# Strassen products of a feed-forward layer accumulated onto one another in PSUM

## The chip, the cores and the metric

The kernel runs on one core of a Trainium2 chip. The metric is the device time of one execution in microseconds (us). Five engines take part: TensorE (PE in the profile; its weight loads are PEld), VectorE (DVE), ScalarE (ACT), GpSimd (POOL) and SyncE (SP), which issues the transfers.

## The reference

One layer of a streaming encoder: a half-step feed-forward, token mixers, a second half-step feed-forward and a final norm, over 1024 + 64 tokens of width 1024. The change touches only the feed-forward parts:

```python
def swiglu(h, w_up, w_down):
    a, b = jnp.split(h @ w_up, 2, axis=-1)
    return (jax.nn.silu(a) * b) @ w_down
...
    x = x + 0.5 * g1 * swiglu(modulate(rms_norm(x, norm_f1), sh1, sc1), w_up1, w_down1)
...
    x = x + 0.5 * g2 * swiglu(modulate(rms_norm(x, norm_f2), sh2, sc2), w_up2, w_down2)
```

D_FF is 2816, that is 22 blocks of 128 columns each in `a` and in `b`.

## The kernel before, in words

**Numbers.** All products are in fp32 precision made from two parts: each operand is split into `hi` (a cast on ScalarE, line 134) and `lo` (source minus hi, line 138, on VectorE or GpSimd), and `mm3` issues three matmuls, hi·hi, hi·lo, lo·hi (lines 162, 163, 164).

**Stages.** FFN1 takes the span up to about 890 us, the mixers and their merge up to about 1870 us, FFN2 the rest. Each feed-forward runs over two groups of tokens, g = 0 (512 tokens, in halves of c = 256 columns) and g = 1 (576 tokens, c = 288).

**up(j).** For each of the 22 blocks j, `up(j)` computes a 2x2 block product in Strassen's (Winograd's) form: seven products, 0 to 6, of 12 matmuls each (4 steps k, three matmuls each). Its weights come from `pair_weights`: two blocks are loaded, sums of their halves formed (`ws` tiles), and four sets split: `wa` from the loaded block, `ws` and `wt` from the sums, `wb` from half a block. In the profile all are called whi and wlo (whi<-raw is wa; whi<-ws is ws or wt) except wb. Three buffers each exist for whi and wlo. The lists LOES say which engine makes each lo part: in both feed-forwards VectorE makes those of ws and wt, and GpSimd those of wa and of the down weights (`wd`). Each product is put into a PSUM bank of its own (pool misc, 6 banks; a tile here is called misc), and `add` (line 510, VectorE) combines the banks with tiles in SBUF called t: seven adds `t<-misc,t`, a copy of product 0 on ScalarE (line 577), two Silu on ScalarE (lines 586 and 593, SBUF to SBUF), and two multiplications `v<-t` of two SBUF tiles, also at line 510.

**down.** After every second block `down` multiplies two finished blocks with two blocks of w_down (wd) into banks (pools acc, 2 banks, and misc) and adds each to x on VectorE (line 632). 512 columns per matmul in g = 0, 288 in g = 1.

**Order.** The code's order is not the engines' order: a scheduler places the instructions on each engine's queue ahead of the run, and each engine works its queue in order, waiting on semaphores. PSUM banks go to whatever tile comes next when free.

Of the kernel before, what the change touches and what calls it, by code (L numbers as in the profile page):

```python
# [26 lines left out]
NF = DFF // P  # L27
# [16 lines left out]
NY, NV, NTT, SIDE0, SIDE, TAIL, SLACK, NRA, NS0, WAIT, NNEAR = 4, 2, 8, 7, 3, 2, 5, 3, 3, 1, 2  # L44
# [39 lines left out]
def encoder_layer(tc: tile.TileContext, a, o, stage=9):  # L84
    nc = tc.nc
# [18 lines left out]
    def slot(i):  # L104

        return hpool.tile([P, 1152], F32R, tag=f"h{i}", name=f"h{i}")
# [25 lines left out]
    def split(src, hi, lo, eng=None):  # L132

        nc.scalar.copy(hi, src)  # L134
        if eng is None:
            rr[0] += 1
            eng = nc.gpsimd if rr[0] % 3 else nc.vector
        eng.tensor_tensor(out=lo, in0=src, in1=hi.bitcast(F32), op=ALU.subtract)  # L138

    def wraw():  # L140
        return wpool.tile([P, KT, P], F32, tag="raw", name="raw", bufs=2)
# [14 lines left out]
    def load_cols(w, c0):  # L156
        return load_w((w[:, c0:c0 + P].rearrange("(k p) c -> p k c", p=P), lambda t: t))

    def mm3(out, w, x, first, last):

        (wh, wl), (xh, xl) = w, x
        nc.tensor.matmul(out, wh, xh, start=first, stop=False)  # L162
        nc.tensor.matmul(out, wh, xl, start=False, stop=False)  # L163
        nc.tensor.matmul(out, wl, xh, start=False, stop=last)  # L164

    V, G = nc.vector, nc.gpsimd
    LOE, SE = [], []
# [146 lines left out]
    def group(n):  # L314

        g = n // 2
        b0 = BLK[n][0] - GRP[g][0]
        return g, slice(b0, b0 + BLK[n][1])
# [147 lines left out]
    def run(*gens):  # L466
        for g in gens:
            for _ in g:
                pass
# [36 lines left out]
    def flat(t):  # L506
        return t.rearrange("p k c -> p (k c)")

    def add(out, in0, in1, op=ALU.add, eng=nc.vector):
        eng.tensor_tensor(out=out, in0=in0, in1=in1, op=op)  # L510
# [23 lines left out]
    def products(g, hs, ws, bank, pump):  # L534

        c = GRP[g][1] // 2

        def product(i):
            t = bank()[:, :c]
            (wh, wl), half = ws[i]  # L540
            for k in range(4):
                mm3(t, (wh[:, 4 * half + k], wl[:, 4 * half + k]), [q[:, k * c:(k + 1) * c] for q in hs[i]], k == 0, k == 3)
            pump(i)
            return t

        return product
# [7 lines left out]
    def up_weights(w_up, j):  # L554
        return pair_weights(w_up, j * P, DFF + j * P, lambda: kviews(fraw()[:, :D]), new_ws)

    def ffn(g, x, hs, w_up, w_down, gate, fpool, npool, after, after_n, side=iter(()), tail=(), first=None):

        G = 2
        gs = {}  # L560
        ln = GRP[g][1]
        c = ln // 2

        def tmp():
            return npool.tile([P, 288], F32, tag="t", name="t", bufs=NTT)[:, :c]

        def up(j, n):

            def pump(i):
                for _ in range(n * (i + 1) // 7 - n * i // 7):  # L570
                    next(side, None)

            early = j == 0 and first is not None
            ws = first if early else up_weights(w_up, j)
            product = products(g, hs, ws, misc, pump)
            p1, u2, u4 = tmp(), tmp(), tmp()
            nc.scalar.copy(p1, product(0))  # L577
            y0, t = p1, None
            if early:
                t, y0 = product(2), tmp()  # L580
                add(y0, product(3), p1)
            add(u2, product(1), p1)
            add(u4, product(2) if t is None else t, u2)
            if not early:
                add(y0, product(3), p1)
            nc.scalar.activation(y0, y0, AF.Silu)
            c22, u3 = tmp(), u2
            p7 = product(4)
            add(c22, p7, u4)
            add(u3, p7, u2)  # L590
            y1 = u4
            add(y1, product(5), u4)
            nc.scalar.activation(y1, y1, AF.Silu)  # L593
            c21 = u3
            add(c21, product(6), u3)
            v = npool.tile([P, 576], F32, tag="v", name="v", bufs=NV)
            add(v[:, c:ln], c22, y1, ALU.mult)
            add(v[:, :c], c21, y0, ALU.mult)
            gt = slot(14 + j % 3) if j % 3 < 2 else fpool.tile([P, 1152], F32R, tag="g", name="g", bufs=1)
            gs[j] = gt[:, :ln], gt[:, ln:2 * ln]  # L600
            if j < NF - 1:
                split(v[:, :ln], *gs[j], nc.gpsimd)
                return
            for cs in (slice(c, ln), slice(0, c)):
                hi, lo = (t[:, cs] for t in gs[j])
                (nc.scalar.copy if cs.start else nc.vector.tensor_copy)(hi, v[:, cs])
                nc.vector.tensor_tensor(out=lo, in0=v[:, cs], in1=hi.bitcast(F32), op=ALU.subtract)

        def down(js, last):
            wd = []  # L610
            for j in js:
                raw = wraw()
                nc.sync.dma_start(flat(raw), w_down[j * P:(j + 1) * P, :])
                w = [fpool.tile([P, KT, P], F32R, tag=f"wd{i}", name="wd", bufs=2) for i in range(2)]
                split(raw, *w, LOE[4])
                wd.append(w)
            work = [iter(tail)]
            if last:
                parts = [(n, group(n)[1]) for n in BGRP[g]]
            else:  # L620
                parts = [(None, slice(c0, c1)) for c0, c1 in ([(0, 512)] if g == 0 else [(0, 288), (288, 576)])]
            items = [(n, cs, m) for n, cs in parts for m in range(KT)]
            for q0, q1 in [(0, 6)] * last + [(q, q + 1) for q in range(6 * last, len(items))]:
                banks = [(acc if m % 4 == 0 else misc)()[:, :cs.stop - cs.start] for n, cs, m in items[q0:q1]]
                for i, j in enumerate(js):
                    for t, (n, cs, m) in zip(banks, items[q0:q1]):
                        mm3(t, (wd[i][0][:, m], wd[i][1][:, m]), [q[:, cs] for q in gs[j]], i == 0, i == len(js) - 1)
                for t, (n, cs, m) in zip(banks, items[q0:q1]):
                    for s, c0, c1 in ((0, cs.start, min(cs.stop, 512)), (1, max(cs.start, 512), cs.stop)):
                        if c0 < c1:  # L630
                            xm = x()[:, m, c0:c1]
                            nc.vector.scalar_tensor_tensor(out=xm, in0=t[:, c0 - cs.start:c1 - cs.start],  # L632
                                                           scalar=gate()[:, m, s:s + 1], in1=xm,
                                                           op0=ALU.mult, op1=ALU.add)
                    if last:
                        after(n, m)
                        for _ in range(TAIL):
                            while work and next(work[0], work) is work:
                                work.pop(0)
                    if last and m == KT - 1:  # L640
                        work.append(iter(after_n(n)))
            return chain(*work)

        groups = [list(range(j, min(j + G, NF))) for j in range(0, NF, G)]
        pend = None
        for js in groups:
            for q, j in enumerate(js):
                up(j, SIDE0 if j < NS0 and not g else SIDE)
                if q == 0 and pend is not None:
                    down(pend, False)  # L650
                    pend = None
            pend = js
        run(side)
        return down(pend, True)

# [83 lines left out]
    hs = [None] * 7  # L739
# [19 lines left out]
    first = up_weights(a["w_up1"][0], 0)  # L759
# [50 lines left out]

    args = a["w_up1"][0], a["w_down1"][0], lambda: ycol["g1"], fpool, npool, after1, lambda n: ()
    run(ffn(0, lambda: xg[0], hs, *args, side_work(), fetch_sums(hs, far1), first))
    new_x(1)
    w_in, early_w = a["w_in"][0], {}
# [36 lines left out]
    def c4():  # L851
        return dec["pool"].tile([P, dec["c4"]], F32, tag="c4", name="c4", bufs=NC4)
# [433 lines left out]
    def fill(g, mt, dst):  # L1286

        fs = ft(), ft()
        yield from pair(g, mt, mt + 1, *fs)
        for f, d in zip(fs, dst):  # L1290
            nc.sync.dma_start(part2(d, GRP[g]), f[:, :GRP[g][1]])
# [9 lines left out]
    for g in range(2):  # L1301
# [38 lines left out]
        rest = deque(fills)  # L1340
# [6 lines left out]
        while lins or rest:  # L1347
            if lins and live[0] + lins[0][0] <= dec["u"]:
                n, f, i = lins.popleft()
                live[0] += n  # L1350
                gen = f(g, i)
            elif rest:
                gen = fill(g, *rest.popleft())
# [15 lines left out]
    if stage == 2:  # L1369
        for h in range(HEADS):  # L1370
            t = c4()
            nc.sync.dma_start(t, osp_a[h])
            nc.sync.dma_start(o["dbg_x"][:, h], t)
            t = c4()
# [101 lines left out]
    hs = [None] * 7  # L1476
# [90 lines left out]
```

## Time and profile before

| | |
|---|---|
| time, median of 3 runs | 2633.03 us (2632.71 to 2633.3) |
| profiled execution | 2635.21 us, span 2633.4 us, mean granted clock 0.974 |
| busy, share of the span | PE 94%, PEld 87%, DVE 76%, POOL 62%, ACT 41% |
| matmuls | 17278 |

The span runs from the first to the last instruction of the profiled execution; its time of 2635.21 us is 1.8 us longer. Busy time counts instructions in work. The granted clock is the share of the full TensorE clock that the chip gave.

### The profile page before, as it was taken

To read this page: it belongs to the slowest core of one execution; us is meant where nothing else is said; L and a number is where in the kernel's file an instruction comes from. 1 tells how busy PE (TensorE), PEld (TensorE's weight loads), DVE (VectorE), ACT (ScalarE), POOL (GpSimd) and SP (SyncE) were. 2 spreads that over 40 slices of the span, in tenths; PEclk is the share of its full clock that TensorE was granted. 3 is DMA by queue.
4 is the path that set the end of the run, shared out by engine and by line. 5 is a ranking of instruction groups with operands and counts; after the bars stand their busy time and mean duration, and the time that the engine had idled before them with its cause. 6 is when DMAs were issued, how large, how long until landed. Compare 5 with 4: busy or idle time off the path is not lost. (4 is left out here: it accounts for less than half of the span.)

```text
span 2633.4 us, 45325 instructions
## 1 busy us (share of the span) xinstructions
PE 2483.8 (94%) x17278; PEld 2278.7 (87%) x17278; DVE 2000.4 (76%) x3276; ACT 1074.2 (41%) x1715; POOL 1630.4 (62%) x977
## 2 busy tenths in 40 slices
PE   6999998999999879998999999999799999999998
PEld 3788888999999768887888887799699998999998
DVE  6787778877667898888765665546888888877776
ACT  4443334343333443444434435534343444333333
POOL 4787666777665656677444543656767665665663
PEclk9999999999999889999999999999799999999999
DMA  8654445444443553444333335646533335323321
GB/s 274 217 179 147 153 145 182 134 144 145 137 126 111 173 163 119 155 137 127 108 111 100 120 95 182 219 129 189 158 97 100 109 106 171 120 89 91 94 82 44
DMA packets 423853, 360.78 MB, mean 137 GB/s; under 512 B 19676, under 2 KB 359316, under 8 KB 423636
## 3 DMA queue, kind: packets, MB, share of 16 engines
q1 hardware_dynamic: 423456, 357.83, 43.7%
q8 instruction: 136, 2.23, 0.4%
q14 instruction: 81, 0.66, 0.1%
q10 hardware_dynamic: 180, 0.06, 0.0%
HBM read 303.50 MB, written 52.10 MB: 135 GB/s over the span
## 5 line engine op out<-in xcount | busy, mean ns | idle before, releaser
L162 PE MATMUL misc<-h,whi 128*128 128x288 f32 (+2 forms) x3360 | 1013.3, 302 | 38.8 <-DVE t L510 18.8
L164 PE MATMUL misc<-h,wlo 128*128 128x288 f32 (+2 forms) x3360 | 987.8, 295 | 9.4 <-DVE wlo L138 8.9
L163 PE MATMUL misc<-h,whi 128*128 128x288 f32 (+2 forms) x3360 | 991.6, 295 | 4.3 <-DVE h L138 4.3
L162 PEld LDWEIGHTS misc<-h,whi 128*128 128x128 f32 x3360 | 647.2, 193 | 90.0 <-DVE t L510 28.5
L164 PEld LDWEIGHTS misc<-h,wlo 128*128 128x128 f32 x3360 | 646.4, 193 | 17.6 <-DVE wlo L138 10.2
L163 PEld LDWEIGHTS misc<-h,whi 128*128 128x128 f32 x3360 | 647.8, 193 | 13.2 <-DVE h L138 6.1
L510 DVE TENSOR_TENSOR t<-misc,t 128x256 f32<-128x256 f32 (+1 forms) x736 | 307.5, 432 | 263.1 <-PE misc L164 239.2
L138 POOL TENSOR_TENSOR wlo<-raw,whi 128x1024 fp32r<-128x1024 f32 x150 | 373.7, 2491 | 200.7 <-ACT whi L134 179.7
L138 DVE TENSOR_TENSOR wlo<-ws,whi 128x1024 fp32r<-128x1024 f32 x178 | 331.6, 1863 | 71.9 <-ACT whi L134 71.8
L138 POOL TENSOR_TENSOR wd<-raw,wd 128x1024 fp32r<-128x1024 f32 x88 | 210.8, 2416 | 152.1 <-ACT wd L134 152.1
L510 POOL TENSOR_TENSOR ws<-raw 128x512 f32<-128x512 f32 x134 | 193.3, 1445 | 123.8 <-DVE wlo L138 81.8
L134 ACT CAST whi<-ws 128x1024 fp32r<-128x1024 f32 x178 | 186.4, 1047 | 176.8 <-PE misc L163 116.1
L632 DVE SCALAR_TENSOR_TENSOR x<-misc,gate,x 128x64 f32<-128x64 f32 (+3 forms) x540 | 237.0, 483 | 23.5 <-PE misc L164 22.7
L134 ACT CAST whi<-raw 128x1024 fp32r<-128x1024 f32 x160 | 167.4, 1046 | 202.8 <-PE misc L163 158.5
L162 PE MATMUL misc<-h,wd 128*128 128x288 f32 (+3 forms) x552 | 180.9, 333 | 7.6 <-DVE t L510 6.9
L510 DVE TENSOR_TENSOR v<-t 128x288 f32<-128x288 f32 (+1 forms) x176 | 182.6, 1050 | 1.7 <-ACT t L593 1.6
L163 PE MATMUL misc<-h,wd 128*128 128x288 f32 (+3 forms) x552 | 181.7, 330 | 0.0
L164 PE MATMUL misc<-h,wd 128*128 128x288 f32 (+3 forms) x552 | 180.1, 329 | 0.0
L510 POOL TENSOR_TENSOR h<-raw 128x512 f32<-128x512 f32 x78 | 110.1, 1411 | 85.1 <-issue 40.1
L134 ACT CAST wd<-raw 128x1024 fp32r<-128x1024 f32 x88 | 88.4, 1048 | 167.7 <-PE misc L163 157.2
L162 PE MATMUL misc<-h,wb 128*128 128x256 f32 (+1 forms) x512 | 151.0, 295 | 1.9 <-ACT t L577 1.7
L163 PE MATMUL misc<-h,wb 128*128 128x256 f32 (+1 forms) x512 | 148.4, 290 | 0.0
(295 smaller groups left out, 4922.7 us busy)
## 6 DMA issues: line engine op xcount, KB each, us to landing
raw<-in_w_up_dram SPq DMA_DIRECT2D x176, 512.0 KB, 4.0
raw<-in_w_down_dram SPq DMA_DIRECT2D x88, 512.0 KB, 3.5
raw<-in_w_in_dram SPq DMA_DIRECT2D x80, 512.0 KB, 4.0
rawa<-in_w_ada_dram SPq DMA_DIRECT2D x88, 256.0 KB, 3.8
h<-in_w_ada_dram SPq DMA_DIRECT2D x16, 512.0 KB, 7.2
raw<-in_w_o_dram SPq DMA_DIRECT2D x16, 512.0 KB, 4.6
raw<-far SPq DMA_DIRECT2D x14, 576.0 KB, 3.8
rawy<-in_w_ada_dram SPq DMA_DIRECT2D x24, 256.0 KB, 5.0
```

What stands on the lines that cost most here:

```text
L134: nc.scalar.copy(hi, src)
L138: eng.tensor_tensor(out=lo, in0=src, in1=hi.bitcast(F32), op=ALU.subtract)
L162: nc.tensor.matmul(out, wh, xh, start=first, stop=False)
L163: nc.tensor.matmul(out, wh, xl, start=False, stop=False)
L164: nc.tensor.matmul(out, wl, xh, start=False, stop=last)
L510: eng.tensor_tensor(out=out, in0=in0, in1=in1, op=op)
L632: nc.vector.scalar_tensor_tensor(out=xm, in0=t[:, c0 - cs.start:c1 - cs.start], scalar=gate()[:, m, s:s + 1], in1=xm, op0=ALU.mult, op1=AL ...
```

## The change

Products that Strassen's form adds are now added by TensorE: a product may be accumulated onto a bank that already holds another. The order of the seven products becomes 0, 3, 1, 4, 2, 5, 6, in three banks: `one` takes 0, then 1, 2 and 5; `y0` takes 3; `five` takes 4, then 6. Between two products that go onto the same bank ScalarE copies the partial sum to SBUF (p1 behind 0, u2 behind 1, u4 behind 2). VectorE keeps three adds (y0 in its bank, c22 = five + u4, c21 = five + u2). Silu is applied in the bank, so the two multiplications read one SBUF tile and one bank. Line numbers move: the copies are lines 583, 593 and 602, Silu 590 and 610, the update of x 650. Block j = 0 of FFN1's first group has its weights ahead and a fourth bank.

`up` has become a generator: `begin(j + 1)` (the next block's weights and its product 0) is placed ahead of the remainder of block j.

```diff
-    def mm3(out, w, x, first, last):
+    def mm3(out, w, x, first, last, onto=False):
...
-        nc.tensor.matmul(out, wh, xh, start=first, stop=False)
+        nc.tensor.matmul(out, wh, xh, start=first, stop=False, skip_group_check=onto)
...
-        def product(i):
-            t = bank()[:, :c]
+        def product(i, t=None):
+            onto = t is not None
+            if not onto:
+                t = bank()[:, :c]
             (wh, wl), half = ws[i]
             for k in range(4):
-                mm3(t, (wh[:, 4 * half + k], wl[:, 4 * half + k]), [q[:, k * c:(k + 1) * c] for q in hs[i]], k == 0, k == 3)
+                mm3(t, (wh[:, 4 * half + k], wl[:, 4 * half + k]), [q[:, k * c:(k + 1) * c] for q in hs[i]],
+                    k == 0 and not onto, k == 3, onto)
...
-            p1, u2, u4 = tmp(), tmp(), tmp()
-            nc.scalar.copy(p1, product(0))
-            y0, t = p1, None
+            p1, u2, u4, c22 = (tmp() for _ in range(4))
+            c21 = p1
+            one = product(0)
+            nc.scalar.copy(p1, one)
+            yield
             if early:
-                t, y0 = product(2), tmp()
-                add(y0, product(3), p1)
-            add(u2, product(1), p1)
-            add(u4, product(2) if t is None else t, u2)
-            if not early:
-                add(y0, product(3), p1)
+                three = product(2)
+                yield
+            y0 = product(3)
+            add(y0, y0, p1)
             nc.scalar.activation(y0, y0, AF.Silu)
-            c22, u3 = tmp(), u2
-            p7 = product(4)
-            add(c22, p7, u4)
-            add(u3, p7, u2)
-            y1 = u4
-            add(y1, product(5), u4)
+            yield
+            product(1, one)
+            nc.scalar.copy(u2, one)
+            yield
+            if early:
+                add(u4, three, u2)
+                five = product(4)
+            else:
+                five = product(4)
+                yield
+                product(2, one)
+                nc.scalar.copy(u4, one)
+            add(c22, five, u4)
+            yield
+            if early:
+                y1 = product(5, three)
+                add(y1, y1, u2)
+            else:
+                y1 = product(5, one)
             nc.scalar.activation(y1, y1, AF.Silu)
-            c21 = u3
-            add(c21, product(6), u3)
             v = npool.tile([P, 576], F32, tag="v", name="v", bufs=NV)
             add(v[:, c:ln], c22, y1, ALU.mult)
+            yield
+            product(6, five)
+            add(c21, five, u2)
             add(v[:, :c], c21, y0, ALU.mult)
...
+        def begin(j):
+            gen = up(j, SIDE0 if j < NS0 and not g else SIDE) if j < NF else iter(())
+            next(gen, None)
+            return gen
...
+        pend, gen = [], begin(0)
+        for j in range(NF):
+            for _ in range(4):
+                next(gen)
+            gen, rest = begin(j + 1), gen
+            run(rest)
+            if j % G == 0 and pend:
+                down(pend, False)
+                pend = []
+            pend.append(j)
```

What the scheduler makes of it shows in three queues, at the same place of FFN2's second group: around an odd block j, beside which the weights of a coming `down` and of block j + 1 are made ready.

**VectorE before**, from the end of a `down` (updates of x) through one block: wlo is the lo part of ws, then of wt; t are the sums of Strassen's form.

```order
L632 SCALAR_TENSOR_TENSOR x<-misc,gate_18897,x 128x64
L510 TENSOR_TENSOR t<-misc,t 128x288 x3
L138 TENSOR_TENSOR wlo<-ws,whi 128x1024
L510 TENSOR_TENSOR t<-misc,t 128x288 x2
L510 TENSOR_TENSOR ws<-raw 128x512
L510 TENSOR_TENSOR t<-misc,t 128x288
L510 TENSOR_TENSOR ws<-ws,raw 128x512
L138 TENSOR_TENSOR wlo<-ws,whi 128x1024
L510 TENSOR_TENSOR t<-misc,t 128x288
L510 TENSOR_TENSOR v<-t 128x288 x2
```

**VectorE now**, same place: the first `misc<-misc,t` is the add of y0; the first `t<-misc,t` is c22 = five + u4.

```order
L650 SCALAR_TENSOR_TENSOR x<-misc,gate_18634,x 128x64
L510 TENSOR_TENSOR misc<-misc,t 128x288
L138 TENSOR_TENSOR wlo<-ws,whi 128x1024
L510 TENSOR_TENSOR t<-misc,t 128x288
L510 TENSOR_TENSOR ws<-raw 128x512
L510 TENSOR_TENSOR ws<-ws,raw 128x512
L138 TENSOR_TENSOR wlo<-ws,whi 128x1024
L510 TENSOR_TENSOR v<-t,misc 128x288
L510 TENSOR_TENSOR t<-misc,t 128x288
L510 TENSOR_TENSOR v<-t,misc 128x288
```

Four adds of a bank are gone, and c22 stands behind the lo part of the next block's ws.

**ScalarE before**, same place, from the casts of the down weights.

```order
L134 CAST wd<-raw 128x1024 x2
L577 COPY t<-misc 128x288
L134 CAST whi<-raw 128x1024
L134 CAST whi<-ws 128x1024
L586 ACTIVATE t<-t 128x288
L134 CAST whi<-ws 128x1024
L593 ACTIVATE t<-t 128x288
L134 CAST wb<-raw 128x512
```

**ScalarE now**: line 602 is the copy of u4, line 593 that of u2.

```order
L593 COPY t<-misc 128x288
L134 CAST wd<-raw 128x1024 x2
L134 CAST whi<-raw 128x1024
L590 ACTIVATE misc<-misc 128x288
L134 CAST whi<-ws 128x1024
L602 COPY t<-misc 128x288
L134 CAST whi<-ws 128x1024
L610 ACTIVATE misc<-misc 128x288
L134 CAST wb<-raw 128x512
```

The cast of the next block's wa follows the two casts of wd directly, and the copy of u4 stands behind the cast of the next block's ws.

**TensorE before**, same place: the end of product 4 (operand h_24455) and the start of product 5 (h_24461), each in a bank of its own.

```order
L162 MATMUL misc<-h_24455,whi 128x288
L163 MATMUL misc<-h_24456,whi 128x288
L164 MATMUL misc<-h_24455,wlo 128x288
L162 MATMUL misc<-h_24461,whi 128x288
L163 MATMUL misc<-h_24462,whi 128x288
L164 MATMUL misc<-h_24461,wlo 128x288
```

**TensorE now**: the last matmul of product 2 (h_24047), what stands between, and the start of product 5 (h_24066), both onto `one`. Product 6 follows product 5's twelve matmuls directly.

```order
L164 MATMUL misc<-h_24047,wlo 128x288
L162 MATMUL acc<-h_27568,wd 128x288
L163 MATMUL acc<-h_27568,wd 128x288
L162 MATMUL acc<-h_27568,wd 128x288
L163 MATMUL acc<-h_27568,wd 128x288
L162 MATMUL misc<-h_24034,whi 128x288
L163 MATMUL misc<-h_24035,whi 128x288
L162 MATMUL misc<-h_24053,whi 128x288
L163 MATMUL misc<-h_24054,whi 128x288
L164 MATMUL acc<-h_27568,wd 128x288 x2
L162 MATMUL misc<-h_24066,whi 128x288
L163 MATMUL misc<-h_24067,whi 128x288
```

Between product 2 and product 5 stand ten matmuls, the first ones of the coming `down` and of block j + 1.

## Rows read from the trace of the kernel before

**Rows 1.** The page: busy time by engine, and the granted clock in 40 slices.

```profile
PE 2483.8 (94%) x17278; PEld 2278.7 (87%) x17278; DVE 2000.4 (76%) x3276; ACT 1074.2 (41%) x1715; POOL 1630.4 (62%) x977
...
PEclk9999999999999889999999999999799999999999
```

**Rows 2.** Windows of the two feed-forward parts: busy time by engine, granted clock, DMA.

```profile
200.00:432.00 232.00, 231.89 (x1616) 207.67 (x1616) 173.99 (x226) 90.59 (x129) 160.79 (x93) 1.00 0.46 143
432.00:600.00 168.00, 151.71 (x1074) 148.19 (x1073) 137.23 (x222) 68.75 (x103) 125.17 (x77) 0.95 0.52 161
620.00:850.00 230.00, 230.00 (x1730) 218.95 (x1729) 155.47 (x303) 81.91 (x115) 139.00 (x81) 1.00 0.42 131
1960.00:2195.00 235.00, 235.00 (x1619) 219.85 (x1617) 198.52 (x258) 96.27 (x139) 157.96 (x90) 1.00 0.33 100
2195.00:2320.00 125.00, 114.38 (x836) 111.52 (x835) 105.29 (x165) 51.84 (x81) 79.28 (x44) 0.97 0.46 145
2320.00:2590.00 270.00, 270.00 (x2032) 270.00 (x2031) 213.72 (x381) 100.84 (x141) 166.22 (x93) 1.00 0.28 86
```

**Rows 3.** Waits of TensorE: engine, line, what ended them; total us, times, longest.

```profile
PE misc L162 <- DVE t L510: 27.7, 16, 6.5
...
PE misc L164 <- DVE wlo L138: 8.9, 6, 2.6
```

**Rows 4.** VectorE by line and shape, window 2320 to 2590 (FFN2, second group).

```profile
L138 DVE TENSOR_TENSOR wlo<-ws,whi 128x1024 fp32r<-128x1024 f32 x32 | 59.3, 1853 | 8.7 <-ACT whi L134 8.7
L510 DVE TENSOR_TENSOR t<-misc,t 128x288 f32<-128x288 f32 x111 | 48.5, 449 | 44.8 <-PE misc L164 43.9
L510 DVE TENSOR_TENSOR v<-t 128x288 f32<-128x288 f32 x32 | 35.1, 1115 | 0.0
```

**Rows 5.** Timeline of VectorE, 2400 to 2442: start, duration, instruction, [idle before].

```profile
2409.05 1.21 DVE L138 TENSOR_TENSOR wlo<-ws,whi 128x1024 fp32r<-128x1024 f32 x1
...
2427.67 1.92 DVE L138 TENSOR_TENSOR wlo<-ws,whi 128x1024 fp32r<-128x1024 f32 x1 [0.54 <-ACT whi L134]
```

**Rows 6.** Timeline of GpSimd, same stretch.

```profile
2420.88 4.78 POOL L138 TENSOR_TENSOR wd<-raw,wd 128x1024 fp32r<-128x1024 f32 x2 [5.14 <-ACT wd L134]
2426.11 2.40 POOL L138 TENSOR_TENSOR wlo<-raw,whi 128x1024 fp32r<-128x1024 f32 x1 [0.45 <-ACT whi L134]
```

**Rows 7.** Timeline of ScalarE, same stretch.

```profile
2419.75 2.00 ACT L134 CAST wd<-raw 128x1024 fp32r<-128x1024 f32 x2 [5.85 <-PE misc L163]
2421.87 0.40 ACT L577 COPY t<-misc 128x288 f32<-128x288 f32 x1
...
2426.59 1.05 ACT L134 CAST whi<-ws 128x1024 fp32r<-128x1024 f32 x1 [0.56 <-PE misc L163]
```

**Rows 8.** Timeline of TensorE, 2418 to 2430: the end of a down, product 0, product 1.

```profile
2419.42 0.29 PE L163 MATMUL misc<-g,wd 128*128 128x288 f32 x1
...
2421.54 0.29 PE L164 MATMUL misc<-h,wlo 128*128 128x288 f32 x1
2421.67 0.30 PE L162 MATMUL misc<-h,whi 128*128 128x288 f32 x1
```

**Rows 9.** VectorE by line and shape, window 1960 to 2195 (FFN2, first group).

```profile
L138 DVE TENSOR_TENSOR wlo<-ws,whi 128x1024 fp32r<-128x1024 f32 x30 | 63.6, 2120 | 15.3 <-ACT whi L134 15.3
L510 DVE TENSOR_TENSOR t<-misc,t 128x256 f32<-128x256 f32 x105 | 41.6, 414 | 20.8 <-PE misc L164 17.7 <-ACT h L134 2.2
```

**Rows 10.** Timeline of TensorE, 2004.5 to 2007: 512 columns, then sixteen of 256.

```profile
2004.82 0.39 PE L164 MATMUL misc<-h,wd 128*128 128x512 f32 x1
2005.05 0.28 PE L162 MATMUL misc<-h,whi 128*128 128x256 f32 x1
...
2006.96 0.28 PE L163 MATMUL misc<-h,whi 128*128 128x256 f32 x1
```

**Rows 11.** Windows with short idle stretches of TensorE, and the clock.

```profile
440.00:464.00 24.00, 19.25 (x124) 18.17 (x124) 23.65 (x30) 11.52 (x21) 17.98 (x9) 0.88 0.73 235
500.00:540.00 40.00, 39.10 (x295) 38.63 (x293) 33.18 (x58) 13.17 (x19) 30.44 (x19) 1.00 0.32 97
```

More of the change, by code (lines that the diff above doesn't have):

```diff
@@ L157, in load_cols @@
         return load_w((w[:, c0:c0 + P].rearrange("(k p) c -> p k c", p=P), lambda t: t))
-    def mm3(out, w, x, first, last):
+    def mm3(out, w, x, first, last, onto=False):
         (wh, wl), (xh, xl) = w, x
-        nc.tensor.matmul(out, wh, xh, start=first, stop=False)
-        nc.tensor.matmul(out, wh, xl, start=False, stop=False)
-        nc.tensor.matmul(out, wl, xh, start=False, stop=last)
+        nc.tensor.matmul(out, wh, xh, start=first, stop=False, skip_group_check=onto)
+        nc.tensor.matmul(out, wh, xl, start=False, stop=False, skip_group_check=onto)
+        nc.tensor.matmul(out, wl, xh, start=False, stop=last, skip_group_check=onto)
     V, G = nc.vector, nc.gpsimd
@@ L642, in down @@
             return chain(*work)
[L644 to L652, printed above, removed]
+        def begin(j):
[12 more added lines that the diff above has]
+            pend.append(j)
         run(side)
```

## The prediction

> **What bounds the kernel now.** I read the page first: TensorE is busy 94% of the span, VectorE 76%, and the granted clock is at or near full in nearly every slice [rows 1]. A change that takes no matmul away can therefore win only where TensorE stands still. The windows say where that is [rows 2]: in the steady stretches of three of the four feed-forward groups (620 to 850, 1960 to 2195, 2320 to 2590) TensorE is busy all the time at a clock of 1.00, and in the fourth (200 to 432) for 231.89 of 232 us. VectorE, busy 68 to 84% there, delays nobody. Idle time lies at the joins of the stages: 16.3 us in 432 to 600 and 10.6 us in 2195 to 2320. The list of what TensorE waits for [rows 3] has two entries that VectorE's load in the feed-forward could explain: 27.7 us on the adds t and 8.9 us on wlo. So the most that a lighter VectorE can give is 36.6 us, all at joins.
>
> **What is removed.** For each of the 87 blocks of the new form VectorE loses four adds of a bank, 0.449 us each in the second group and 0.414 in the first [rows 4, 9]. The two multiplications shrink: with both inputs in SBUF they take 1.115 us on average [rows 4]. With one input in PSUM I price them like the nearest form, the adds t<-misc,t, at 0.449; were only half of that gain real, nothing below would move, since they stand behind the chain that I cost. Together 4 x 0.449 + 2 x 0.666 = 3.1 us a block, some 270 us of VectorE's 2000. In the steady stretches this is worth nothing, since TensorE is the cover and already full. At the joins it is worth between 0 and 36.6 us; I take a third of the 26.9 us of idle time in the two windows, rounded down to **8 us**, since what ends many of those waits is not a removed instruction.
>
> **What is added on ScalarE.** Two more copies a block, 0.40 us each [rows 7], 70 us in all. ScalarE is busy 100.84 of 270 us [rows 2], so its load hides; where the copies stand in its queue matters.
>
> **What is added as order.** Formerly a product went into a free bank, and nothing on TensorE waited for its sum. Now product 5 may not start before u4 is copied out of `one`, and product 6 not before VectorE has formed c22 out of `five`, which itself needs u4. Call T the moment at which TensorE could start what follows product 2. In the even blocks 5.2 us or more of other matmuls lie between T and product 6. In the odd ones, at the place shown in the three queues, there are ten matmuls up to product 5 and twelve more up to product 6. At the spacing of 0.133 us [rows 8] that is **1.33 us and 2.93 us** in FFN2's second group. In its first group it is six of 512 columns (0.23 us) and four of 256 (0.12) up to product 5, twelve of 256 on top: 1.84 and **3.28 us** [rows 10]. In FFN1's second group product 6 has 3.37 us in six blocks and 2.93 in two, in its first group about 5.0.
>
> Now the chain behind T. ScalarE starts 0.20 us after the matmul that releases it (2421.87 against 2421.67) [rows 7, 8]. The cast of the next ws is released one matmul before T, so it runs from T + 0.07 to T + 1.12 (1.05 us) [rows 7]; the copy of u4 follows until T + 1.52. Product 5 is thus 0.2 us late at most. On VectorE the lo part of ws stands ahead of c22 and is ready at T + 1.15 (0.03 us behind the cast) [rows 5, 7]. It takes 1.21 us when it runs alone. It took 1.92 us at 2427.67, when GpSimd was in a subtraction from 2426.11 to 2428.51: it ended 1.08 us after GpSimd [rows 5, 6]. So a VectorE instruction with two SBUF inputs waits for GpSimd's running one and then takes 1.08 us; the adds with a bank do not show this, their mean is 0.449 [rows 4].
>
> Is GpSimd in work at T + 1.15? It works off the two wd lo parts and then that of the next wa. The first cast of wd is released by the last matmul with the old wd's hi part, which the cast follows by 0.20 us (2419.75 against 2419.42 + 0.13) [rows 7, 8]. In FFN2's second group 38 matmuls lie from there to T (four of the down, 24 of products 3 and 4, ten of product 2), 5.04 us. The cast runs from T - 4.84 to T - 3.79, GpSimd starts 0.08 later, needs 4.78 us for the two wd [rows 6] and begins wa's at **T + 1.07**, 0.08 us ahead of VectorE. It ends at T + 3.47, VectorE's wlo at T + 4.55, c22 at T + 5.00. Product 6 was due at T + 2.93: TensorE stands for **2.0 us**. In FFN2's first group (four of 512 and 36 of 256 columns, 5.23 us) GpSimd begins at T + 0.88, ends at T + 3.28, wlo at T + 4.36, c22 at T + 4.78 against 3.28: **1.5 us**. In FFN1's second group (40 matmuls, 5.31 us) it begins at T + 0.80, and c22 ends at T + 4.73 against 3.37: **1.36 us**. In FFN1's first group the gap of 5.0 us covers it: nothing.
>
> The Trainium skill, "SBUF — State Buffer", section "Who interferes with whom", says that whoever issues first holds the shared port for the whole instruction and that the other fully blocks. By that rule a lead of 0.08 us is as good as one of 1.56 us, which is the lead in rows 5 and 6; if instead such a short lead does not count, the 2.0 us fall away.
>
> The sum: 9 odd blocks x 2.0 in FFN2's second group, 9 x 1.5 in its first, 6 x 1.36 in FFN1's second group, and two blocks there with a gap of 2.93 us whose GpSimd I have not placed, between 0 and 1.8 us, 0.9 each: 18 + 13.5 + 8.2 + 1.8 = 41.5 us. Less the 8 us at the joins: +34 us. The profiled execution would go from 2635.2 to 2669 us; the median of the runs is 2.2 us lower, so I say **2667 us**.
>
> **Rivals.** *Blocked in all three groups* is the forecast (0.44), 2655 to 2680 us: the relief at the joins between 0 and 20 us.
>
> *VectorE comes first, everything fits* (0.24). If GpSimd is later than I place it, VectorE's wlo begins at T + 1.15 and takes 1.21 us; c22 ends at T + 2.81, before product 6 is due in any group. What is left is product 5, 0.2 us x 9 = 1.7 us. With the relief of 8 us the median becomes 2633 - 8 + 2 = 2627 us, faster. It decides at a shift of 0.08, 0.28 and 0.35 us in the three groups, hand-overs that I know to about 0.05 us each in a chain of five. For it speaks also that wlo's mean in FFN2's second group is 1.853 us, so about half of them are hardly held [rows 4].
>
> *No relief either* (0.12). As the last, but the waits at the joins only change their names, since copies now stand where adds stood: 2633 + 2 = 2635 us, no change.
>
> *Only the short margin fails* (0.11). FFN2's second group falls out of the sum: 34 - 18 + 2 = +18, 2651 us.
>
> *The clock falls as well* (0.09). In 440 to 464, where TensorE stood for 4.75 us of 24, the clock was 0.88; in 500 to 540, with 0.9 of 40 idle, it stayed 1.00 [rows 11]. The new stalls, 2 us in every 35, lie between. If the nine longest each cost as much as a stretch of 24 us at 0.88 (24 x 0.12 = 2.9 us), 26 us are added: 2693 us. The Trainium skill, "TensorE: Matmul & The Clock Gate", section "A second HAM failure mode: psum-queue depth-cycling", describes short pauses of TensorE between groups of matmuls that cycle through banks and let the clock swing; rows 11 show it for long pauses alone.
>
> **Numbers.** A measurement of this kernel can tell about 0.2% (5 us) from no change. Slower: 0.44 + 0.11 + 0.09 = 0.64; same 0.12; faster 0.24. The range must reach the fast rival, and on the other side most of the way to the clock's: 2624 to 2686 us. The likeliest case alone has 2655 to 2680.
>
> **What the profile after would show.** Right: TensorE's wait on `t` of line 510 at product 6 rises from 27.7 to some 65 us, in 24 or more pieces of 1.3 to 2.1 us, one per odd block; before each of them VectorE's wlo of about 3.4 us, GpSimd's wlo<-raw beginning just ahead of it; steady windows in which TensorE is no longer busy all the time (about 18 us idle in 2320 to 2590 moved by the delay). The multiplications at 0.45 us and VectorE's busy time down by about 250 us. Wrong: VectorE's wlo behind product 2 at 1.21 us, TensorE full in the steady windows, and a shorter span from fewer waits at the joins. The forecast also fails if the sums in the bank cost TensorE's matmuls anything: their spacing must stay at 0.133 us.

## The result

The changed kernel takes **2695.24 us** (median of 4 runs, 2692.02 to 2698.97) against 2633.16 us before: a ratio of 1.0234, 95% interval 1.0216 to 1.0252. It is slower by 62 us, almost twice the 34 us of the forecast and above its range. The profiled execution took 2692.02 us, its span is 2690.2 us, 56.8 us longer than before. The page of the changed kernel, by engine and clock, answers to [rows 1]:

```profile
PE 2520.1 (94%) x17278; PEld 2275.2 (85%) x17278; DVE 1706.1 (63%) x2926; ACT 1125.6 (42%) x1890; POOL 1582.7 (59%) x977
...
PEclk9999999899999999998999999998899999999999
```

The matmuls are as many as before (17278), the clock is no lower, and VectorE lost 294 us of busy time, as the change intends. TensorE, however, is *busy* 36 us longer. That is the line to stop at: the same instructions took more of TensorE's time.

Three windows of each kernel, cut at TensorE's last matmul of the last product 6 of FFN1 and of the first product 6 of FFN2, place the difference. The columns are the stretch, its length, busy time (and instructions) of TensorE, its weight loads, VectorE, ScalarE and GpSimd, then the granted clock, the DMA share and GB/s. Before:

```profile
0.00:866.70 866.70, 817.50 (x5735) 742.78 (x5736) 646.79 (x1004) 342.83 (x502) 587.78 (x353) 0.98 0.51 161
866.70:1859.20 992.50, 928.66 (x6266) 823.21 (x6265) 725.26 (x1294) 432.39 (x765) 566.39 (x352) 0.97 0.46 141
1859.20:2633.40 774.20, 737.66 (x5281) 712.67 (x5279) 628.32 (x981) 298.95 (x450) 476.19 (x274) 0.98 0.34 105
```

After:

```profile
0.00:904.70 904.70, 855.27 (x5750) 746.62 (x5751) 508.00 (x833) 368.08 (x592) 572.51 (x353) 0.98 0.50 155
904.70:1890.20 985.50, 922.10 (x6263) 816.45 (x6262) 715.89 (x1285) 431.36 (x768) 570.77 (x355) 0.97 0.46 142
1890.20:2690.20 800.00, 742.75 (x5269) 712.08 (x5267) 482.23 (x809) 326.16 (x533) 439.43 (x271) 0.98 0.33 101
```

FFN1 is 38 us longer, the mixers between, whose code the change leaves alone, 7 us shorter, FFN2 26 us longer. In FFN1 TensorE's busy time grows by 37.8 us and its idle time stays at 49 us (30 of the 37.8 us are placed below); in FFN2 the idle time grows from 36.5 to 57.3 us. These are two different losses.

**FFN2: the stall that was forecast.** The waits of TensorE (total us, times, longest):

```profile
PE misc L162 <- DVE t L510: 47.2, 36, 6.2
PE misc L164 <- DVE wlo L138: 14.6, 6, 5.5
...
PE misc L162 <- DVE v L510: 9.6, 4, 3.5
```

The adds `t` now cost 47.2 us in 36 waits, against 27.7 in 16 [rows 3]. One of them, in FFN2's second group, follows engine by engine. T is, as in the prediction, the moment at which TensorE could start what follows product 2. TensorE: product 5 (whi) begins, ends, and product 6 (wb) begins:

```profile
2438.33 0.40 PE L162 MATMUL misc<-h,whi 128*128 128x288 f32 x1
...
2439.91 0.29 PE L164 MATMUL misc<-h,wlo 128*128 128x288 f32 x1
2441.72 0.40 PE L162 MATMUL misc<-h,wb 128*128 128x288 f32 x1 [1.52 <-DVE t L510]
```

VectorE, lo part of ws and c22:

```profile
2438.02 3.28 DVE L138 TENSOR_TENSOR wlo<-ws,whi 128x1024 fp32r<-128x1024 f32 x1 [3.47 <-ACT whi L134]
2441.22 0.45 DVE L510 TENSOR_TENSOR t<-misc,t 128x288 f32<-128x288 f32 x1
```

GpSimd, the second wd and wa's lo part:

```profile
2435.45 2.41 POOL L138 TENSOR_TENSOR wd<-raw,wd 128x1024 fp32r<-128x1024 f32 x1
2437.81 2.41 POOL L138 TENSOR_TENSOR wlo<-raw,whi 128x1024 fp32r<-128x1024 f32 x1
```

ScalarE, cast of ws and copy of u4:

```profile
2436.93 1.05 ACT L134 CAST whi<-ws 128x1024 fp32r<-128x1024 f32 x1 [1.59 <-PE misc L163]
2437.89 0.39 ACT L602 COPY t<-misc 128x288 f32<-128x288 f32 x1
```

The cast of ws, released one matmul ahead of T, puts T at 2436.86. GpSimd begins wa's lo part at T + 0.95, VectorE arrives at T + 1.16, 0.21 us behind it, and is held until GpSimd ends at 2440.22; it ends 1.08 us later, c22 0.37 after that. Product 6 stood ready behind product 5 at 2440.04 and starts at 2441.72: 1.68 us lost. (The page counts idle time from the modelled end of a matmul, so it shows 1.52; distances from start to start, less the 0.13 us of a matmul, are used below.)

**FFN1: something else.** The modulation vectors are computed beside FFN1, by matmuls of 32 columns of weights, four at a time into four strips of 32 rows of a bank (line 293). Each shows as two records. TensorE before, such a group in the first group of FFN1:

```profile
270.08 0.62 PE L293 MATMUL misc<-rawy,ct 128*32 128x512 f32 x1
270.09 0.63 PE L293 MATMUL misc<-rawa,ct 128*32 128x512 f32 x3
270.54 0.59 PE L293 MATMUL misc<-rawy,ct 128*32 128x512 f32 x1
270.55 0.60 PE L293 MATMUL misc<-rawa,ct 128*32 128x512 f32 x3
271.08 0.38 PE L162 MATMUL misc<-h,whi 128*128 128x256 f32 x1
```

Eight records start within half a microsecond and the next matmul follows 1.00 us after the first. Every one of the 24 groups before looks like this: 23.9 us in all. The changed kernel, one matmul of such a group alone:

```profile
275.31 1.04 PE L293 MATMUL misc<-rawa,ct 128*32 128x512 f32 x2
276.29 0.38 PE L162 MATMUL misc<-h,whi 128*128 128x256 f32 x1
```

One matmul, two records, 0.98 us. Call a stretch of such matmuls with no other matmul between them a *run*. In the changed kernel the same 96 matmuls stand in 55 runs of one to four, each of 0.97 to 1.00 us: 53.9 us. That is **30.0 us** more of TensorE's time, with not one matmul more.

VectorE's groups in the steady stretch 2370 to 2646 answer to [rows 4]:

```profile
L138 DVE TENSOR_TENSOR wlo<-ws,whi 128x1024 fp32r<-128x1024 f32 x29 | 49.8, 1717 | 35.5 <-ACT whi L134 35.5
...
L510 DVE TENSOR_TENSOR t<-misc,t 128x288 f32<-128x288 f32 x30 | 13.5, 450 | 0.0
L510 DVE TENSOR_TENSOR v<-t,misc 128x288 f32<-128x288 f32 x30 | 13.5, 448 | 0.3
```

The multiplications take 0.448 us, as priced.

### The profile page after: what moved, and what is told of

Read it like the earlier page. It is cut to its first block, busy times and chain, and to the rows that moved or that the text cites. A ratio compares the mean times of both kernels' runs of the same rounds, so it can differ in the third digit from the quotient of the medians.

```text
span 2690.2 us, 44956 instructions
## 1 busy us (share of the span) xinstructions
PE 2520.1 (94%) x17278; PEld 2275.2 (85%) x17278; DVE 1706.1 (63%) x2926; ACT 1125.6 (42%) x1890; POOL 1582.7 (59%) x977
## 3 DMA queue, kind: packets, MB, share of 16 engines
q1 hardware_dynamic: 423456, 357.83, 43.1%
## 4 chain that ended last, share of the span: by engine, by line
PE 44%; DVE 5%; DMA 1%; ACT 1%; issue 1%; POOL 1%; SPq 0%; DVEq 0%; ACTq 0%; POOLq 0%
PE misc L162 12%; PE misc L164 12%; PE misc L163 11%; DVE wlo L138 3%; PE S L1088 1%; PE acc L163 1%; PE acc L162 1%; PE acc L164 1%; PE misc L1111 1%; ACT whi L134 1%; DVE h L138 1%; PE misc L1192 1%; PE misc L1176 1%; PE misc L1200 0%; PE misc L1125 0%
## 5 line engine op out<-in xcount | busy, mean ns | idle before, releaser
L162 PE MATMUL misc<-h,whi 128*128 128x288 f32 (+2 forms) x3360 | 1012.1, 302 | 43.1 <-DVE t L510 14.0
L138 DVE TENSOR_TENSOR wlo<-ws,whi 128x1024 fp32r<-128x1024 f32 x178 | 289.2, 1625 | 293.6 <-ACT whi L134 283.4
L510 POOL TENSOR_TENSOR ws<-raw 128x512 f32<-128x512 f32 x134 | 182.2, 1361 | 211.6 <-DVE wlo L138 123.7
L650 DVE SCALAR_TENSOR_TENSOR x<-misc,gate,x 128x64 f32<-128x64 f32 (+3 forms) x540 | 247.9, 489 | 83.9 <-PE misc L164 82.7
L138 POOL TENSOR_TENSOR wb<-raw,wb 128x512 fp32r<-128x512 f32 x44 | 59.4, 1349 | 233.9 <-ACT wb L134 233.9
L163 PE MATMUL misc<-h,wd 128*128 128x288 f32 (+3 forms) x552 | 180.2, 327 | 0.0
L164 PE MATMUL misc<-h,wd 128*128 128x288 f32 (+3 forms) x552 | 178.4, 326 | 0.0
L162 PE MATMUL misc<-h,wd 128*128 128x288 f32 (+3 forms) x552 | 176.8, 329 | 0.0
L650 DVE SCALAR_TENSOR_TENSOR x<-acc,gate,x 128x64 f32<-128x64 f32 (+3 forms) x180 | 83.8, 487 | 135.3 <-PE acc L164 135.0
L510 DVE TENSOR_TENSOR t<-misc,t 128x256 f32<-128x256 f32 (+1 forms) x297 | 128.5, 433 | 61.7 <-PE misc L164 49.2
```

The lines of the kernel that those rows point to most:

```text
L162: nc.tensor.matmul(out, wh, xh, start=first, stop=False, skip_group_check=onto)
L163: nc.tensor.matmul(out, wh, xl, start=False, stop=False, skip_group_check=onto)
L164: nc.tensor.matmul(out, wl, xh, start=False, stop=last, skip_group_check=onto)
```

## The experiments

The unit of comparison is the kernel before, timed in the same job (2632.9 to 2634.9 us). "Stalls ahead of product 6" are those over 0.4 us; in the changed kernel 9 of 1.41 and one of 0.42 us in FFN2's first group, 8 of 1.68 to 1.70 in its second, 7 of 0.82 to 1.41 from the end of FFN1's first group through its second; 33.4 us in all.

**x1_together.** The modulation matmuls of a step become ready together.

```diff
-            for m in range(4):
-                nc.tensor.matmul(t[32 * m:32 * m + 32, :], ct[:, n % 2 * 4 + m, :], raws[m], start=(n % 2 == 0),
+            lt = fpool.tile([P, 4, 32], F32, tag="lt", name="lt", bufs=1)
+            nc.vector.scalar_tensor_tensor(out=lt.rearrange("p m c -> p (m c)"), in0=raws[3][:, :128], scalar=0.0,
+                                           in1=ct[:, n % 2 * 4:n % 2 * 4 + 4, :].rearrange("p m c -> p (m c)"),
+                                           op0=ALU.mult, op1=ALU.add)
+            for m in (1, 2, 3, 0):
+                nc.tensor.matmul(t[32 * m:32 * m + 32, :], lt[:, m, :], raws[m], start=(n % 2 == 0),
                                  stop=(n % 2 == 1))
```

> The changed kernel, with the four modulation matmuls of a step (32 columns of weights each, into four strips of one bank) made ready at the same moment, by a small VectorE instruction that reads the last of their four loads; on TensorE's queue they then stand in 31 separate runs in place of 55 (24 before the change). Theory A, the part of the loss that the prediction did not have is the splitting of these runs, each of which costs about 0.98 us however many of the four it holds: 24 x 0.98 = 23.5 us less, 2672 us. Rival B, the splitting is harmless and the whole loss is waiting behind partial sums: 2690 to 2700 us. The stalls ahead of product 6 (1.41, 1.70 and about 0.87 us) stay under both.

Measured: 2683.76 us, ratio 1.019 (1.0165 to 1.0214), 11 us less than the changed kernel and between the times of the two theories. In the trace the runs take 30.7 us in place of 53.9, as theory A has it, and FFN1's last product 6 comes at 883 in place of 905 us, 22 us earlier. The stalls in FFN2 are the same but for the one of 0.42 us (12.7 and 13.5 us in its two groups); in FFN1 they sum to 5.3 us in place of 6.8, four of 0.86 to 1.01 us having come at other places and the second group's six having gone. But the mixers take 1002 us in place of 985, with 92 us of their time at the lower clock in place of 61. The price of the runs is confirmed in its stage; the whole gained half of it.

**x9_together24.** As x1, with the modulation steps placed behind the products by a product's place in the new order, so that the matmuls stand in 24 runs.

```diff
-            pump(i)
+            pump((0, 2, 4, 1, 3, 5, 6)[i])
```

> The changed kernel with the modulation matmuls made ready together and their steps called by a product's place in the new order, so that they stand in 24 runs of four as before the change; GpSimd keeps wa's lo part. Theory A, the split runs cost 30 us (53.9 against 23.9 us of TensorE's time) and the stalls ahead of product 6 about 33 us, independent of each other: the first feed-forward ends some 28 us earlier than in the changed kernel, the stalls of 1.41 and 1.70 us in the second stay, 2665 us; a further gain or loss in the mixers, where no instruction is changed, would be the clock's. Rival B, the version with 31 runs gained only 11 us because the price of a run is half of what I take it for: 2680 us, and the first feed-forward ends only 15 us earlier.

Measured: 2689.29 us, ratio 1.0207 (1.0182 to 1.0233). Both theories miss the time. The runs do take 23.9 us, but FFN1 is only 12 us shorter than in the changed kernel. Two of TensorE's waits show where it went:

```profile
PE misc L297 <- DVE lt L293: 7.5, 6, 1.8
...
PE acc L162 <- ACT h L134: 5.9, 5, 1.7
```

The first is TensorE waiting for `lt`, which waits for the last of four loads, the second for a cast of h at the start of a `down`, four of the five in FFN1. In the changed kernel TensorE has no wait on the modulation loads that the profile lists, and 1.7 us of the second kind. The gathering instruction also stands in VectorE's queue, which works in order: VectorE waits 98.2 us in 22 places for the last load (104.6 us in 23 in x1), and what stands behind it there waits too. So these two runs show the price of the split and a side effect of the gathering together, and of the 30 us gathering alone gave back 22 us of FFN1 in x1 and 12 here. Which loss came from which wait was not taken apart.

**x3_one_strip.** The kernel before, with the four matmuls in one strip.

```diff
-                nc.tensor.matmul(t[32 * m:32 * m + 32, :], ct[:, n % 2 * 4 + m, :], raws[m], start=(n % 2 == 0),
-                                 stop=(n % 2 == 1))
+                nc.tensor.matmul(t[:32, :], ct[:, n % 2 * 4 + m, :], raws[m], start=(n % 2 == 0 and m == 0),
+                                 stop=(n % 2 == 1 and m == 3))
...
-            nc.scalar.copy(mrow, t)
+            nc.scalar.copy(mrow[:32], t[:32])
...
-                nc.tensor.matmul(t[:, 2 * q:2 * q + 2], mrow[:, q * P:(q + 1) * P], sel, start=True, stop=True)
+                nc.tensor.matmul(t[:, 2 * q:2 * q + 2], mrow[:32, q * P:(q + 1) * P], sel[:32], start=True, stop=True)
```

> The kernel before, with the four modulation matmuls of a step put one after the other into one strip of 32 rows of the bank, in place of four strips; the same number of matmuls, in the same 24 runs of four. Theory A, a run of four costs as little as one matmul because the four go into different strips and run at the same time: 24 x 3 x 0.98 = 70 us more, 2703 us, and a run lasts 3.9 us in place of 1.0. Rival B, what makes them cheap is that they stand together in the queue: no change, 2633 us.

Measured: 2696.91 us, ratio 1.0244 (1.0221 to 1.0266), 64 us more. TensorE, one group, by timeline:

```profile
200.67 1.05 PE L293 MATMUL misc<-rawy,ct 128*32 128x512 f32 x2
201.56 2.74 PE L293 MATMUL misc<-rawa,ct 128*32 128x512 f32 x6
```

Four matmuls still stand together, and take 3.55 us on average in place of 1.0: 85.2 us in 24 runs, 61 us more. Theory A holds, with 0.9 us for a matmul in the same strip: standing together is not enough, the neighbours save because they go into different strips and run at the same time.

**x2_wa_dve.** The lo part of wa goes to VectorE.

```diff
-    LOES = [[G, V, V, V, G], [G, V, G, V, V], [G, V, V, G, G]]
+    LOES = [[V, V, V, V, G], [G, V, G, V, V], [V, V, V, G, G]]
```

> The changed kernel with the lo part of wa on VectorE in both feed-forwards, in place of GpSimd. Theory A, VectorE's lo part of ws ahead of c22 is held by GpSimd's lo part of wa: with that gone the stall ahead of product 6 falls from 1.41, 1.70 and 0.87 us to at most 0.3 us, though VectorE has one more subtraction of 1.2 us in the same queue ahead of c22: about 27 us less. The runs of modulation matmuls also fall to 31: 23 us less. Together 2645 us. Rival B, what delays c22 is the length of VectorE's and ScalarE's own queue: the stalls stay or grow by 1.2 us each, 2670 to 2700 us.

Measured: 2640.03 us, ratio 1.0026 (1.0014 to 1.0039), 55 us less than the changed kernel and 5 us below theory A. No stall over 0.4 us is left ahead of product 6 in three of the four groups; one of 2.3 us came up in the other. VectorE at the same place, with wa's lo part (wlo<-raw) now in its own queue ahead:

```profile
2393.53 1.58 DVE L138 TENSOR_TENSOR wlo<-raw,whi 128x1024 fp32r<-128x1024 f32 x1 [0.48 <-ACT whi L134]
2396.79 1.67 DVE L138 TENSOR_TENSOR wlo<-ws,whi 128x1024 fp32r<-128x1024 f32 x1 [1.68 <-ACT whi L134]
2398.38 0.45 DVE L510 TENSOR_TENSOR t<-misc,t 128x288 f32<-128x288 f32 x1
```

The lo part of ws takes 1.67 us in place of 3.28, though 1.58 us of VectorE's work were added in front of it. Rival B falls: the queue was longer and the stall went. The modulation matmuls stand in 31 runs, as expected, but take 44.2 us: six runs hold a fifth matmul, which goes into a strip that the run has used already, and take 1.83 us each; in six others of two or three the matmuls start one behind the other, the first ones behind their loads, and the run takes 1.65 to 3.67 us.

**x5_wa_halves.** GpSimd makes wa's lo part in two instructions.

```diff
-        split(ra, *wa, LOE[0])
+        nc.scalar.copy(wa[0], ra)
+        for q in (slice(0, 4), slice(4, 8)):
+            LOE[0].tensor_tensor(out=wa[1][:, q], in0=ra[:, q], in1=wa[0][:, q].bitcast(F32), op=ALU.subtract)
```

> The changed kernel with GpSimd's lo part of wa made by two instructions of half the size (the same work). Theory A, VectorE's lo part of ws waits for the one GpSimd instruction that is in work when it arrives, so half an instruction holds it 1.2 us less: the stall ahead of product 6 falls from 1.41 to about 0.2, from 1.70 to about 0.5 and from 0.87 to 0 us, 27 us less. The runs of modulation matmuls stand in 38 pieces: 17 us less. Together 2651 us. Rival B, VectorE waits for GpSimd's work as a whole or for something else: stalls unchanged, 2678 us.

Measured: 2639.63 us, ratio 1.0023 (1.0012 to 1.0033), 12 us better than expected. The stalls over 0.4 us are gone in all groups. VectorE (ws, then c22) and GpSimd (two wd, then the two halves), at the same place:

```profile
2396.28 1.92 DVE L138 TENSOR_TENSOR wlo<-ws,whi 128x1024 fp32r<-128x1024 f32 x1 [3.74 <-ACT whi L134]
2398.12 0.44 DVE L510 TENSOR_TENSOR t<-misc,t 128x288 f32<-128x288 f32 x1
```

```profile
2391.12 4.76 POOL L138 TENSOR_TENSOR wd<-raw,wd 128x1024 fp32r<-128x1024 f32 x2 [4.51 <-ACT wd L134]
2395.83 3.53 POOL L523 TENSOR_TENSOR wlo<-raw,whi 128x512 fp32r<-128x512 f32 x2
```

VectorE is held for 0.7 us only, until the first half ends, and then goes ahead of the second: the two halves of GpSimd together need 3.53 us, since now GpSimd waits. At this place work, engines and order are the same; only the length of the instruction that holds VectorE changed (elsewhere the scheduler's order moved too, as the 38 modulation runs show). Of the 12 us beyond the expectation 6 are stalls (33 us of them went, not 27), while the runs gave 11 us for the 17 expected (43.1 us in 38 runs). What is left over I put down to VectorE's relief, which would be seen once the stalls are gone: FFN2 takes 767 us against 774 before the change, and FFN1 12.5 us more than before, though its modulation runs take 19 us more. No run shows that reading by itself.

**x4_silu_bank.** One part of the change alone, in the kernel before.

```diff
...
             if not early:
-                add(y0, product(3), p1)
+                y0 = product(3)
+                add(y0, y0, p1)
...
-            y1 = u4
-            add(y1, product(5), u4)
+            y1 = product(5)
+            add(y1, y1, u4)
```

> The kernel before (seven banks, order 0 to 6, no accumulation) with one part of the change alone: y0 and y1 are summed and put through Silu in their banks, and the two multiplications read one bank and one SBUF tile. Theory A, VectorE's load is not what bounds the steady stretches, but at the joins it is: v falls from about 1.05 to 0.45 us, some 100 us of VectorE's busy time go, and the time falls by 5 to 10 us, 2623 to 2628 us. Rival B, the joins wait for other things: 2633 us, and the 8 us that the prediction took for the relief were wrong.

Measured: 2627.93 us, ratio 0.9983 (0.9973 to 0.9993), 5 us less: theory A, at its upper edge. VectorE's busy time fell by 106 us and the multiplications to 0.41 and 0.44 us. By stages FFN1 took 8 us and FFN2 5 us less, the mixers 6 us more.

**x8_no_overlap.** Without the overlap of neighbouring blocks.

```diff
-            gen, rest = begin(j + 1), gen
-            run(rest)
+            run(gen)
...
             pend.append(j)
+            gen = begin(j + 1)
```

> The changed kernel without the overlap of neighbouring blocks: the next block begins behind the last product of this one. Everything else stays, also c22 behind the lo part of ws on VectorE. Theory A, the overlap causes neither loss: the stalls ahead of product 6 remain, by the new gaps to product 6 (about 2.6 and 4.0 us in FFN2's two groups in place of 3.3 and 2.9) some 2 us and 0.6 us each, and the modulation matmuls stand in 40 runs in place of 55, 15 us less: about 2675 to 2690 us. Rival B, the overlap brought both: below 2650 us.

Measured: 2675.71 us, ratio 1.0166 (1.0153 to 1.018), where theory A put it, but not by its way. The stalls ahead of product 6 are gone but for two (one of 0.64 us in FFN2, one of 2.28 in FFN1), against my 2 and 0.6 us; in their place stand 0.26 us at each `down` of FFN2's first group and 0.46 us at product 5 in its second, behind the copy of u4. ScalarE again copies product 0 between the casts of wd and of wa, as before the change. The modulation matmuls stand in 40 runs, which I had at 39 us and which took 52.7: again six of five matmuls take 1.83 us each, and six of three 2.24 to 2.52. So the overlap does bring the stalls ahead of product 6, and a split of the modulation matmuls (40 runs against 24 before) is there without it. Which of the instructions that the overlap moves is decisive was not taken apart further.

**x6_both_halves.** x5 and the gathering of x1 (26 runs); `lt` is made as there.

```diff
-            for m in range(4):
-                nc.tensor.matmul(t[32 * m:32 * m + 32, :], ct[:, n % 2 * 4 + m, :], raws[m], start=(n % 2 == 0),
...
+            for m in (1, 2, 3, 0):
+                nc.tensor.matmul(t[32 * m:32 * m + 32, :], lt[:, m, :], raws[m], start=(n % 2 == 0),
...
-        split(ra, *wa, LOE[0])
+        nc.scalar.copy(wa[0], ra)
+        for q in (slice(0, 4), slice(4, 8)):
+            LOE[0].tensor_tensor(out=wa[1][:, q], in0=ra[:, q], in1=wa[0][:, q].bitcast(F32), op=ALU.subtract)
```

> The changed kernel with GpSimd's lo part of wa in two halves and the modulation matmuls of a step made ready together (26 runs in place of 55). Theory A, the two causes add up: the stalls ahead of product 6 stay gone as with the halves alone (2640 us) and 12 runs fewer than there save another 12 to 17 us: 2620 to 2628 us, faster than the kernel before by the relief of VectorE at the joins. Rival B, what one saves is given back elsewhere: 2633 to 2640 us.

Measured: 2633.95 us, ratio 0.9998 (0.9985 to 1.0011): rival B. The runs take 25.8 us, no stalls over 0.4 us are left ahead of product 6, FFN1's last product 6 comes at 867 us, as before the change, but FFN2 takes 774 us, also as before: its start took 4.4 us and the join of its two groups 3.2 us more than with the halves alone. Why was not found.

**x7_both_dve.** x2, the gathering, and the steps by place (24 runs); `lt` is made as in x1.

```diff
-    LOES = [[G, V, V, V, G], [G, V, G, V, V], [G, V, V, G, G]]
+    LOES = [[V, V, V, V, G], [G, V, G, V, V], [V, V, V, G, G]]
...
-                nc.tensor.matmul(t[32 * m:32 * m + 32, :], ct[:, n % 2 * 4 + m, :], raws[m], start=(n % 2 == 0),
+                nc.tensor.matmul(t[32 * m:32 * m + 32, :], lt[:, m, :], raws[m], start=(n % 2 == 0),
...
-            pump(i)
+            pump((0, 2, 4, 1, 3, 5, 6)[i])
```

> The changed kernel with the lo part of wa on VectorE, the modulation matmuls made ready together, and their steps called by a product's place in the new order rather than by its number (24 runs, as before the change). Theory A: the stalls ahead of product 6 are gone, and 20 us of the 44 us in the 31 runs of the version with wa on VectorE alone (2640 us): 2618 to 2625 us. Rival B, the joins lose what is saved: 2633 to 2640 us.

Measured: **2617.65 us**, ratio 0.9942 (0.9928 to 0.9955), the fastest of all, 15 us below the kernel before and at the lower edge of theory A. Its three windows, cut as above:

```profile
0.00:852.60 852.60, 812.71 (x5750) 739.69 (x5751) 566.58 (x901) 368.86 (x590) 508.20 (x309) 0.99 0.52 164
852.60:1851.90 999.30, 932.53 (x6252) 824.90 (x6251) 725.88 (x1290) 432.08 (x766) 560.76 (x351) 0.96 0.46 140
1851.90:2619.00 767.10, 737.35 (x5280) 712.06 (x5279) 515.28 (x851) 325.88 (x534) 379.05 (x230) 0.98 0.35 106
```

FFN1 is 14 us shorter than before the change (853 against 867), FFN2 7 us (767 against 774), the mixers 7 us longer. So the kernel that accumulates in PSUM beats the kernel before once the two side effects are taken away. Whether the same edits (wa's lo part on VectorE, the gathering) would gain anything in the kernel before, without accumulation, was not run; how much of the 15 us is the accumulation's own stays open.

## Why the prediction was wrong

- **"A change that takes no matmul away can therefore win only where TensorE stands still"** was taken the other way as well: that the change could *lose* only where TensorE stands still. This step failed: TensorE's own time for the same matmuls was put at no change. For the modulation matmuls it rose from 23.9 to 53.9 us, since they lost their neighbours in the other strips. The sum had no term for it; x3 shows by itself that the strips run at the same time, x1 the price of the split in the changed kernel (22 us of FFN1 for 23 us of runs). It could have been seen in the new order of TensorE's queue, where line 293 stands in 55 places; I read that queue only at the odd blocks of FFN2, where no such matmul is.
- **The chain behind T** was right, place by place: ws's lo part held by GpSimd's wa, c22 behind it, product 6 late, once per odd block. In sizes: FFN2's first group 1.5 forecast, 1.41 measured (9 times); its second 2.0 against 1.69 (8 times, not 9); FFN1's second 1.36 against 0.82 to 0.91 in five of the six and 1.08 in the other; the sum had two more blocks there, at 0.9 each, and only six show a stall; FFN1's first group, put at nothing, has one of 1.41. In sum 33.4 us for the 41.5 forecast. GpSimd started some 0.1 us earlier than worked out, and its lead over VectorE was 0.21 us where I had 0.08.
- **The lead that decides.** x5 shows that it is the one GpSimd instruction in work that holds VectorE, and x2 that without wa's lo part on GpSimd the stall goes. The Trainium skill, "SBUF — State Buffer", section "Who interferes with whom", has the holder keep the port for a whole instruction; by that rule a lead of 0.21 us is enough, and these traces agree (3.28 us with it, 1.92 when the holding instruction was half as long).
- **The relief at the joins**, 8 us, was not seen in the changed kernel: FFN2 lost 26 us with some 25 us of added stalls ahead of product 6, so nothing was left of it. That the stalls without relief (33.4 us) come out near the net 34 us of the sum is luck: both terms were too large. Where the stalls are absent a gain of that size is seen in most runs, 5 us of the whole in x4 and 6 to 8 us of FFN2 in x2, x5 and x7, but none in x6, so the term stays unproven.
- **VectorE's saving** was right (294 us for the 270 forecast; v at 0.448 us), and so was that the steady stretches give nothing for it.
- **The clock** did not fall in the changed kernel (0.976 against 0.974). This rival is out.

The account of the 56.8 us of span: runs +30.0, stalls ahead of product 6 +31.5 (33.4 less 1.9 that stood there before), mixers -7, the rest +2.

What stays open: the mixers, with unchanged code, took 985 to 1002 us in these programs, with 58 to 92 us of that at the lower of the clock's two levels. The changed kernel's 985 is the shortest of all, 6 us under the next; so a difference taken against its whole time can be up to 16 us off from what the changed stage gained (x1), and the cause was not looked for.

## What to carry to other kernels

Before saying that TensorE's work is unchanged, look through its whole queue for matmuls that share the array: four that run at the same time as neighbours cost up to four times as much when something else gets between them (1.00 us together, 0.98 us each alone). Where a partial sum must be read before the next product may go onto it, write down everything that stands ahead of the reader on its engine, and what another engine's running instruction can do to it; splitting that instruction in two may be the whole cure. A lighter engine that was not the bound gives little, and gives it only if the new order does not make waits of its own.

## What the runs showed of the hardware

- Four fp32 matmuls of 128 rows, 32 columns of weights and 512 moving columns took 1.00 us together in four strips, one alone 0.98 us, four in one strip 3.55 us. The Trainium skill, "TensorEngine Tiling (Array Packing)", section "Key Properties", says that tiles operate independently and can run in parallel; the rows agree, and show that a run whose matmuls start together costs the same whether one strip or four are at work; a fifth matmul, in a strip already used, makes it 1.83 us (x2).
- More work on an engine's queue ahead of a critical instruction made the kernel faster (x2): what counted was not the length of VectorE's queue but which engine was inside a long instruction when VectorE arrived.
- A GpSimd subtraction in two halves let VectorE in between them (1.92 us for VectorE, 3.53 us for both halves).
